# One exponential over both decay blocks, earlier splits, norms and p projection, and three PSUM banks for each of two uses

## The chip, the cores and the metric

The kernel runs on one core of a Trainium2 chip. The metric is the device time of one execution in microseconds (us), smaller is better. The engines named below are PE (TensorE, matrix products), PEld (its weight loads), DVE (VectorE), ACT (ScalarE), POOL (GpSimd) and SP (SyncE, which issues most of the DMAs). Each engine runs its own instructions in the order in which they stand and waits, where it must, for semaphores of the others.

## The reference

One layer of a hybrid decoder over 1024 tokens of width 1024, in float32: a Mamba-2 mixer, a mixture of 64 experts in 8 groups, a per-layer embedding that is projected and gated, and a last RMS norm. Cut to what matters here:

```python
u = rms_norm(x);  z, xBC, dt = split(u @ w_in)            # 1024 x 5152
x, B, C = split(silu(causal_conv4(xBC) + conv_b))          # 32 heads of 64, 4 groups, state 128
acum = cumsum(dt * A) within chunks of 128 tokens
decay = exp(acum[l] - acum[s]) for s <= l;   decay_in = exp(acum)
y = (C B^T * decay) @ (x dt) + (C * decay_in) @ state_in   # then the state goes on to the next chunk
h = x_in + (group_rms_norm((y + D x) * silu(z)) * gnorm) @ w_out
h = h + moe(rms_norm(h))         # top-1 group, top-2 experts in it, gated MLPs with 512 hidden
gate = sigmoid(rms_norm(h) @ ple_w_gate + ple_b_gate)
h = h + gate * (p @ ple_w_proj)  # p: 1024 x 256, ple_w_proj: 256 x 1024
out = rms_norm(h)
```

## The kernel before

**The mixer** (`ssd`, from the start to about 640 us). The tokens are taken in two halves `hf` of 512, and in each the four groups `g` one after the other, which makes eight units. A unit projects ten column tiles t = 0 to 9 of `w_in`: B, C, four of x and four of z. A tile is 128 columns by 512 tokens, made as three products of split float32 operands (`xh wh`, `xl wh`, `xh wl`; L204 to L206) over eight blocks of the inner dimension, so 24 matmuls into a PSUM tile "mm". The weights are split just ahead of them in `proj` by L69 and L70: `wh` is a rounded copy on ACT, `wl` the rest on DVE. `conv_tile` then copies the product out (L278) and runs the convolution, three passes on DVE (L284).

Woven between the tiles of a unit is the scan of the unit before, four chunks c of 128 tokens. The dictionary `plan` says after which tile each step is written: `front(0)`, `front(1)`, `back(0)`, `front(2)`, `back(1)`, `front(3)`, `back(2)` and `back(3)` at t = 0, 1, 2, 3, 4, 5, 6 and 8. A `front` loads the cumulated steps of 8 heads, broadcast to all partitions, from the DRAM scratch `acd` into `ac` (L322, 512 KB), and makes two blocks of 128x1024: `ec` = exp(ac) (L338), and, after `ac` has had each row's own value taken off it in place (L340, eight instructions on DVE), `ac` = exp(ac) (L342). The first, times C (L348), weighs the incoming state; the second, times the masked C B^T (L352), weighs the chunk's own inputs. A `back` multiplies both on PE (L369, L371) into "py", and DVE takes "py" on into `yz` (L382, L384). `ac` has three buffers and `ec` two.

`x_half(hf)` loads the tokens, sums their squares, takes the reciprocal root, spreads it over the columns by a turn on PE (L177), loads the transposed columns, and splits them into `xh` and `xl`. For the second half it is written into t = 3 to 7 of the last unit of the first half. Turned tiles and small products use PSUM tiles "tp"; there are four banks for "mm" and two for "tp".

**The output product and the router** (`out_router`, about 640 to 880 us). It multiplies by `w_out`, and routes the tokens in blocks (`stats`, `turn`, `logits`, then the three parts of `route`: `first`, `second`, `third`). At its end nothing but the last block's routing is left: the counts on PE (L685 to L690, tile "pa"), two packings (L714), a gather of token rows by DMA, and the first spreading products of the experts' stage (L1017, `pc<-S,uh`).

**The experts** (`moe`, about 880 us to the end). Eight groups g are taken in turn. Their weights come in blocks of 1 MB, issued by SP through a ring of buffers and a few spare ones (`yx`, `vx`, `ring2`), and PE multiplies them (L1027, tiles "pgate", "pup", "py"). The per-layer embedding of finished tokens (`ple`) is woven into the next group by `fill`: nine times 128 rows. For each, 1 KB rows of `p` are gathered, turned by PE in two transposes (`turn_p`, L855), and projected half by half (`project_p`, L861); the gate's product is L908. In the group g = 6 two more such projections are written early (`project`), for the last two sets of rows.

Instructions are recorded by a framework that puts each engine's instructions in an order of its own, by priorities; a place in the text does not fix the place in a queue, except under `manual_schedule`.

Of the kernel before, what the change touches and what calls it, by code (L numbers as in the profile page):

```python
# [17 lines left out]
T, D = 1024, 1024  # L18
# [23 lines left out]
class K:  # L42
# [64 lines left out]
    def ssd(self, left, right):  # L107
# [35 lines left out]
        def x_half(hf):  # L143

            ss, rs, *tmp = (wk.tile([128, HC], F32, name=n) for n in ("rs", "rs", "nt0", "nt1", "nt2"))
            cols = []

            def columns():
                for j in range(2):
                    w = wraw.tile([128, KD, 256], F32, name="w").rearrange("p a b -> p (a b)")  # L150
                    w = w.rearrange("p (k t) -> p k t", t=HT)
                    nc.sync.dma_start(w, a["xT"].rearrange("(k p) t -> p k t", p=128)[:, 4 * j:4 * j + 4,
                                                                                      hf * HT:(hf + 1) * HT])
                    cols.extend(w[:, k] for k in range(4))

            for i in range(HC):
                t = hf * HC + i
                xt = (wk.tile([128, D], F32, name="ec") if i == 3 else wk.tile([128, D], F32, name="ac", bufs=3))
                nc.sync.dma_start(xt, a["x"][t * 128:(t + 1) * 128, :])
                if i == HC - 1:  # L160
                    if hf == 0:
                        W.append(load(2 * DI, 2 * DI + 512))
                    columns()
# [14 lines left out]
            rsb = wk.tile([128, HT], F32, name="dT", bufs=1)  # L178
            nc.scalar.activation(rsb, pr.rearrange("p c t -> p (c t)"), AF.Copy)

            def scale(k):
                nc.vector.tensor_mul(cols[k], cols[k], rsb)
# [4 lines left out]
            yield  # L187
# [75 lines left out]
        def proj(w, i, x):  # L263
            wh = wsp.tile([128, KD, 128], F32R, name="wh")
            wl = wsp.tile([128, KD, 128], F32R, name="wl")
            self.split(wh, wl, w[:, :, i * 128:(i + 1) * 128])
            ps = self.ps_mm.tile([128, 512], F32, name="mm")
            mm3(ps, wh, wl, x)
            return ps

        def conv_tile(hf, w, i, x, m):
# [5 lines left out]
            ps = proj(w, i, x)  # L277
# [11 lines left out]
        def project(hf, g):  # L289
            x = X[hf]  # L290
            w = W.pop() if W else load(2 * DI + g * 128, 2 * DI + 512 + g * 128)
            xT, zT = [], zp.tile([128, 4, HT], F32, name="z")
            bT = conv_tile(hf, w, 0, x, 16 + g)
            yield
            cT = conv_tile(hf, w, 1, x, 20 + g)
            U[hf, g] = bT, cT, xT, zT
            yield
            for j in range(2):
                w = load(DI + g * 512 + j * 256)
                for i in range(2):  # L300
                    xT.append(conv_tile(hf, w, i, x, 4 * g + 2 * j + i))
                    yield
            for j in range(2):
                w = load(g * 512 + j * 256)
                for i in range(2):
                    nc.scalar.activation(zT[:, 2 * j + i], proj(w, i, x), AF.Silu)
                    yield

        def scan(hf, g):
# [6 lines left out]
            def front(c):  # L316
# [4 lines left out]
                ac = wk.tile([128, 8, Q], F32, name="ac", bufs=3)  # L321
                nc.sync.dma_start(ac, bass.AP(tensor=acd.tensor, offset=acd[8 * g:8 * g + 1, cg * Q:cg * Q + 1].offset,  # L322
# [89 lines left out]
        X, SZ, U, W = {}, {}, {}, []  # L412
        for i, _ in enumerate(x_half(0)):
# [1045 lines left out]
```

## Time and profile before

| what | value |
|---|---|
| median of 3 runs | 1950.36 us (1946.88 to 1954.07) |
| profiled execution, its own time | 1954.31 us |
| span from its first to its last instruction | 1952.4 us |
| mean granted clock of TensorE | 0.982 of full |
| PE busy | 1848.3 us (95%) |
| DVE busy | 1031.5 us (53%) |
| ACT busy | 749.5 us (38%) |
| moved by DMA | 538.39 MB |

The shares of busy time are means over three stages with different limits, so the profile is read stage by stage: the mixer, the output product with the router, the experts.

### The profile page before, as it was taken

The numbers are of one execution on the slowest core, as the hardware profiler recorded it, in microseconds if no ns is written. First come the engines' busy times: TensorE is split into PE (matmuls) and PEld (weight loads), VectorE is DVE, ScalarE is ACT, GpSimd is POOL, SyncE is SP. The second block draws the span as 40 slices with busy tenths as digits, with TensorE's granted clock in tenths as the row PEclk, the third lists the DMA queues.
The fourth block names the chain that finished last, engine by engine and source line by source line (L and its number), as shares of the span: only waits on it lengthen the run. The fifth ranks groups of instructions, "written<-read, shape, count | busy, mean of one in ns | idle before, by whom it ended". The sixth has DMA issues, their size and how long they took to land.

```text
span 1952.4 us, 23158 instructions
## 1 busy us (share of the span) xinstructions
PE 1848.3 (95%) x8702; PEld 1047.1 (54%) x8702; DVE 1031.5 (53%) x2194; ACT 749.5 (38%) x1040; POOL 182.7 (9%) x276
## 2 busy tenths in 40 slices
PE   6999997999999999979999999999999999999996
PEld 4778775777887678863343333433433334334334
DVE  5497896858988876573341514423325244143223
ACT  5476766557767533322021211312222113122223
POOL 1011110201111031021000000000000000000004
PEclk9999998999999999988999999999999999999998
DMA  7425444345442787956999999999999999998883
GB/s 220 118 75 137 115 134 127 88 97 134 110 110 53 243 294 238 346 195 254 422 421 394 401 421 385 412 412 383 420 382 404 420 373 423 404 375 325 337 322 109
DMA packets 192166, 538.39 MB, mean 276 GB/s; under 512 B 16046, under 2 KB 128688, under 8 KB 143920
## 3 DMA queue, kind: packets, MB, share of 16 engines
q1 hardware_dynamic: 177744, 514.21, 72.0%
q10 hardware_dynamic: 11008, 12.94, 2.0%
q0 software_dynamic: 3296, 9.70, 1.3%
q8 instruction: 70, 1.15, 0.2%
q14 instruction: 48, 0.39, 0.1%
HBM read 520.95 MB, written 17.69 MB: 276 GB/s over the span
## 4 chain that ended last, share of the span: by engine, by line
PE 81%; DMA 7%; DVE 7%; ACT 2%; issue 2%; POOL 1%; SPq 0%; POOLq 0%; ACTq 0%; DVEq 0%
PE pup L1027 11%; PE pgate L1027 11%; PE py L1027 10%; PE mm L206 6%; PE mm L204 6%; PE mm L205 6%; PE pq L908 6%; PE pc L1017 3%; PE mm L505 2%; PE mm L506 2%; PE mm L507 2%; DMA w<-in_w_up_dram 2%; PE pc L861 2%; DMA ac<-acd 2%; PE pc L1090 2%
## 5 line engine op out<-in xcount | busy, mean ns | idle before, releaser
L204 PE MATMUL mm<-xh,wh 128*128 128x512 f32 x640 | 265.6, 415 | 3.3 <-ACT xh L197 2.2
L206 PE MATMUL mm<-xh,wl 128*128 128x512 f32 x640 | 254.5, 400 | 8.4 <-DVE wl L70 8.3
L205 PE MATMUL mm<-xl,wh 128*128 128x512 f32 x640 | 253.9, 397 | 0.3 <-DVE xl L198 0.3
L1027 PE MATMUL pup<-w,XT 128*64 128x512 f32 x1016 | 239.1, 598 | 1.6 <-DMA w<-in_w_up_dram 1.6
L1027 PE MATMUL pgate<-w,XT 128*64 128x512 f32 x1000 | 232.7, 599 | 0.0
L1027 PE MATMUL py<-w,hT 128*64 128x512 f32 (+1 forms) x1024 | 227.1, 586 | 2.1 <-DMA w<-in_w_down_dram 2.1
L70 DVE TENSOR_TENSOR yx<-py,yx 128x512 fp32r<-128x512 f32 (+1 forms) x68 | 44.8, 659 | 234.2 <-ACT yx L69 234.2
L1027 PEld LDWEIGHTS py<-w,hT 128*64 128x64 f32 x1024 | 70.0, 137 | 146.2 <-issue 138.2
L1027 PEld LDWEIGHTS pup<-w,XT 128*64 128x64 f32 x1016 | 72.1, 136 | 141.9 <-issue 131.5
L206 PEld LDWEIGHTS mm<-xh,wl 128*128 128x128 f32 x640 | 122.6, 192 | 38.5 <-DVE wl L70 12.2
L204 PEld LDWEIGHTS mm<-xh,wh 128*128 128x128 f32 x640 | 122.9, 192 | 34.2 <-issue 4.5
L1027 PEld LDWEIGHTS pgate<-w,XT 128*64 128x64 f32 x1000 | 68.7, 137 | 134.2 <-issue 129.6
L205 PEld LDWEIGHTS mm<-xl,wh 128*128 128x128 f32 x640 | 123.0, 192 | 29.9 <-issue 4.3
L908 PE MATMUL pq<-wpg,vx 128*128 128x512 f32 x256 | 123.1, 607 | 0.0
L70 DVE TENSOR_TENSOR wl<-w,wh 128x1024 fp32r<-128x1024 f32 x80 | 97.4, 1220 | 46.4 <-ACT wh L69 46.4
L69 ACT ACTIVATE wh<-w 128x1024 fp32r<-128x1024 f32 x80 | 84.3, 1054 | 72.0 <-PE mm L205 59.4
L284 DVE SCALAR_TENSOR_TENSOR xbc<-raw,convw,xbc 128x512 f32<-128x512 f32 x144 | 109.7, 762 | 3.8 <-ACT xbc L282 2.7
L506 PE MATMUL mm<-wl,yh 128*128 128x512 f32 x256 | 99.3, 398 | 2.0 <-DVE wl L517 1.9
L505 PE MATMUL mm<-wh,yh 128*128 128x512 f32 x256 | 96.0, 402 | 4.8 <-ACT yh L69 4.6
L69 ACT ACTIVATE yx<-py 128x512 fp32r<-128x512 f32 (+1 forms) x68 | 38.9, 572 | 159.4 <-PE py L1027 159.4
L1058 ACT ACTIVATE hT<-pt 128x512 f32<-128x512 f32 x31 | 18.4, 593 | 211.5 <-PE pt L1056 211.5
L507 PE MATMUL mm<-wh,yl 128*128 128x512 f32 x256 | 98.0, 393 | 0.0
(360 smaller groups left out, 2815.6 us busy)
## 6 DMA issues: line engine op xcount, KB each, us to landing
w<-in_w_up_dram SPq DMA_DIRECT2D x127, 1024.0 KB, 9.5
w<-in_w_gate_dram SPq DMA_DIRECT2D x125, 1024.0 KB, 9.1
w<-in_w_down_dram SPq DMA_DIRECT2D x120, 1024.0 KB, 9.5
w<-in_w_in_dram SPq DMA_DIRECT2D x32, 1024.0 KB, 5.6
w<-in_w_out_dram SPq DMA_DIRECT2D x48, 512.0 KB, 5.2
ac<-acd SPq DMA_DIRECT2D x32, 512.0 KB, 9.3
w<-in_w_in_dram SPq DMA_DIRECT2D x16, 512.0 KB, 8.7
yn<-yz SPq DMA_DIRECT2D x32, 256.0 KB, 4.4
```

Of the source, the lines that this page charges most:

```text
L69: self.nc.scalar.activation(dst_h, src, AF.Copy)
L70: self.nc.vector.tensor_sub(dst_l, src, r_(dst_h))
L204: nc.tensor.matmul(ps, lhsT=wh[:, k], rhs=x[0][:, k], start=(k == 0), stop=False)
L205: nc.tensor.matmul(ps, lhsT=wh[:, k], rhs=x[1][:, k], start=False, stop=False)
L206: nc.tensor.matmul(ps, lhsT=wl[:, k], rhs=x[0][:, k], start=False, stop=(k == KD - 1))
L284: nc.vector.scalar_tensor_tensor(o, raw[:, j:j + HT], convw[:, m, j:j + 1], o, op0=OP.mult, op1=OP.add)
L505: nc.tensor.matmul(po[i][hf], lhsT=yh[:, ts], rhs=wh[:, cs], start=(k == 0), stop=False)
L506: nc.tensor.matmul(po[i][hf], lhsT=yh[:, ts], rhs=wl[:, cs], start=False, stop=False)
L507: nc.tensor.matmul(po[i][hf], lhsT=yl[:, ts], rhs=wh[:, cs], start=False, stop=(k == 15))
L908: nc.tensor.matmul(V["pq"], lhsT=V["vT"][:, k], rhs=wpg[:, k, cs], start=(k == 0), stop=(k == KD - 1))
L1017: nc.tensor.matmul(px, lhsT=x[:, k], rhs=G.S[:, i], start=(i == 0 and x is u[i][0]), stop=(i == 1 and x is u[i][1]))
L1027: nc.tensor.matmul(ps[64 * b:64 * b + 64], lhsT=xt(k0 + k, b), rhs=w[b][:, k, cs], start=(k0 + k == 0), stop=(k0 + k == K - 1))
```

## The change

1. **One exponential.** `ac` and `ec` become the two halves of one tile `ae`, with two buffers in place of three and two. The load goes to the `ec` half, the eight subtractions write the `ac` half from it, and one ACT instruction over 128x2048 takes both exponentials.
2. **Early splits.** A generator `weights()` writes the split of tile m+1 right after the matmuls of tile m, ahead of its convolution.
3. **Early norms.** The sum of squares and the reciprocal root are a function of their own, `norms(hf)`; that of the second half is written into t = 2 to 6 of the first unit, and its result is kept in `RB`. `x_half(1)` keeps the load of columns, the scaling and the split, at t = 6 and 7 of the last unit of the first half. A scan's norm and store move from t = 0 and 2 to t = 1 and 3.
4. **Early p projection.** All of `p @ ple_w_proj` is made at the end of `out_router`, in 16 pieces (two float32 matmuls of 128x512 and an ACT copy each), in a PE order written by hand around the last routing steps; eight DMAs store it to the DRAM scratch `ppd`. The experts' stage gathers rows of 4 KB from there and makes no projection; `turn_p`, `project_p` and the two early projections in g = 6 go, as does the tile `wpp`.
5. **PSUM.** "mm" has three banks and "tp" three.

```diff
-                ac = wk.tile([128, 8, Q], F32, name="ac", bufs=3)
-                nc.sync.dma_start(ac, bass.AP(tensor=acd.tensor, ...
+                ae = wk.tile([128, 2, 8, Q], F32, name="ae")
+                ec, ac = ae[:, 0], ae[:, 1]
+                nc.sync.dma_start(ec, bass.AP(tensor=acd.tensor, ...
...
-                ec = wk.tile([128, 8, Q], F32, name="ec")
-                nc.scalar.activation(ec, ac, AF.Exp)
                 for h in range(8):
-                    nc.vector.tensor_scalar(ac[:, h], ac[:, h], acs[:, c, 8 * g + h:8 * g + h + 1], 0.0,
+                    nc.vector.tensor_scalar(ac[:, h], ec[:, h], acs[:, c, 8 * g + h:8 * g + h + 1], 0.0,
                                             op0=OP.subtract, op1=OP.min)
-                nc.scalar.activation(ac, ac, AF.Exp)
+                nc.scalar.activation(ae, ae, AF.Exp)
...
+            wh, wl = ahead.pop() if ahead else next(W)
             ps = self.ps_mm.tile([128, 512], F32, name="mm")
             mm3(ps, wh, wl, x)
+            ahead.extend(w for w in [next(W, None)] if w)
             return ps
...
+                if hf == 0:
+                    rows = norms(1)
+                    for t in (2, 3, 4, 5, 6):
+                        at(t, next, rows)
             if before:
-                at(0, before[2])
-                at(2, before[3])
+                at(1, before[2])
+                at(3, before[3])
...
-                for t in (3, 4, 5, 6, 7):
+                for t in (6, 7):
                     at(t, next, xg)
...
+        pieces = project()
+        with tc.manual_schedule(engines={mybir.EngineType.PE}):
+            for f in side[:-3]:
+                f()
+            for n, f in zip((6, 0, 0), side[-3:]):
+                f() if f is not side[-1] else f(lambda n: [next(pieces, None) for _ in range(n)])
+                for _ in range(n):
+                    next(pieces)
+            for _ in pieces:
+                pass
...
-            self.gather(self.p0, self.a["p"], g)
+            self.gather(self.p0, self.ppd, g)
...
-            nc.vector.tensor_mul(gt, gt, self.project_p(V["pT"], hf, pc_) if pr is None else pr[:, cs])
+            nc.vector.tensor_mul(gt, gt, pr[:, cs])
...
-                    early = [project(vx[:, 1792:], nxt.pr), project(self.p0, cur.pr)]
...
-        self.ps_mm = self.pool("ps_mm", 4, PSUM, ps)
-        self.ps_tp = self.pool("ps_tp", 2, PSUM, ps)
+        self.ps_mm = self.pool("ps_mm", 3, PSUM, ps)
+        self.ps_tp = self.pool("ps_tp", 3, PSUM, ps)
```

How the instructions stand on the engines that this concerns. First, SP's queue around the scan's loads in the second half of the mixer, where the scan of the second-to-last group begins (`ac` and `ae` are the loads, `w` those of `w_in`). Before:

```order
L322 DMA ac_4451<-acd_98 128x8x128
L322 DMA ac_4729<-acd_98 128x8x128
L260 DMA w_4833<-in_w_in_dram 128x8x256
L322 DMA ac_4800<-acd_98 128x8x128
L260 DMA w_4989<-in_w_in_dram 128x8x256
L260 DMA w_5129<-in_w_in_dram 128x8x256
L322 DMA ac_4956<-acd_98 128x8x128
```

Here `ac_4729` to `ac_4956` are the loads of chunks 0, 1 and 2; with three buffers, `ac_4956` takes the buffer of `ac_4451`, the last chunk of the scan before. After:

```order
L334 DMA ae_4659<-acd_98 128x8x128
L260 DMA w_5034<-in_w_in_dram 128x8x256
L334 DMA ae_4752<-acd_98 128x8x128
L260 DMA w_5162<-in_w_in_dram 128x8x256
L334 DMA ae_4906<-acd_98 128x8x128
```

With two buffers, `ae_4906`, chunk 2 again, takes the buffer of `ae_4659`, chunk 0 of the same scan, which is read by the products of `back(0)`.

Next, DVE in the same place, from the end of `back(0)` (its result is py_4888 before, py_4823 after) on. Before:

```order
L382 SCALAR_TENSOR_TENSOR yz_4908<-xbc_4445,dsk_104,py_4888 128x128
L340 TENSOR_SCALAR ac_4956<-ac_4956,acs_2820 128x128
L384 TENSOR_TENSOR yz_4908<-yz_4908,z_4020 128x512
L340 TENSOR_SCALAR ac_4956<-ac_4956,acs_2820 128x128 x7
L346 COPY ed_4983<-ec_4972 128x8
L70 TENSOR_TENSOR wl_4994<-w_4989,wh_4993 128x1024
```

After:

```order
L392 SCALAR_TENSOR_TENSOR yz_4843<-xbc_4401,dsk_104,py_4823 128x128
L350 TENSOR_SCALAR ae_4906<-ae_4906,acs_2774 128x128
L394 TENSOR_TENSOR yz_4843<-yz_4843,z_3980 128x512
L350 TENSOR_SCALAR ae_4906<-ae_4906,acs_2774 128x128 x7
L375 TENSOR_TENSOR st_4975<-st_4821,ed_4777 128x512
L415 TENSOR_TENSOR yz_4203<-yz_4203,tp_4893 128x512
L415 TENSOR_TENSOR yz_4357<-yz_4357,tp_4893 128x512
L415 TENSOR_TENSOR yz_4487<-yz_4487,tp_4893 128x512
L415 TENSOR_TENSOR yz_4576<-yz_4576,tp_4893 128x512
L344 TENSOR_TENSOR xc_4916<-tp_4908,dt_s_2773 128x512
L70 TENSOR_TENSOR wl_4965<-w_4880,wh_4964 128x1024
```

In both, the eight subtractions on the chunk's load stand right behind the rows on the result of `back(0)`; after the change the split of the next tile's weights (`wl_4965`) stands some six instructions behind them.

Last, PE at the end of the router. Before, the last logits are followed by the counts, and the last packing by the spreading products:

```order
L618 MATMUL tp<-wr,uT 128x72 x8
L612 MATMUL tp<-ident,h 128x128 x8
L618 MATMUL tp<-wr,uT 128x72 x8
L688 LDWEIGHTS tris
L688 MATMUL tp<-M,tris 128x72
```

After, six pieces of the p projection stand there:

```order
L667 MATMUL tp<-wr,uT 128x72 x8
L661 MATMUL tp<-ident,h 128x128 x8
L667 MATMUL tp<-wr,uT 128x72 x8
L594 MATMUL mm<-w,wh 128x512 x12
L737 LDWEIGHTS tris
L737 MATMUL tp<-M,tris 128x72
```

Two more pieces stand ahead of each packing, and the last six between the second packing and the spreading products:

```order
L764 LDWEIGHTS at
L764 MATMUL tp<-oms,at 128x104
L594 MATMUL mm<-w,wh 128x512 x12
L1048 MATMUL pc<-S,uh 128x512 x2
L1048 MATMUL pc<-S,ul 128x512
```

So 32 matmuls have moved from the experts' stage to a place between the last logits and the first spreading product. On SP the loads of their operands stand behind the first weights of the experts, and the eight stores to `ppd` ahead of three more weight blocks (`ring2`, `yx` and `vx`).

## Rows read from the trace of the kernel before

**Rows 1.** Busy time of each engine in stretches of the span (start and end in us, length, then PE, PEld, DVE, ACT, POOL busy with the number of instructions; at the end the granted clock of TensorE as a share of full, the busy share of the DMA engines, and GB/s).

```profile
20.00:633.00 613.00, 581.11 (x3144) 459.22 (x3143) 478.54 (x987) 403.23 (x492) 91.00 (x155) 0.97 0.43 111
290.00:331.00 41.00, 27.48 (x132) 21.38 (x131) 25.80 (x76) 24.42 (x30) 3.03 (x4) 0.83 0.40 112
320.00:330.00 10.00, 6.71 (x21) 5.22 (x22) 7.50 (x18) 9.08 (x14) 1.84 (x2) 0.66 0.23 72
450.00:600.00 150.00, 150.00 (x856) 120.01 (x855) 130.13 (x261) 107.80 (x130) 24.00 (x28) 1.00 0.44 111
860.00:890.00 30.00, 15.75 (x80) 9.78 (x81) 21.25 (x82) 7.87 (x14) 9.92 (x19) 0.66 0.40 137
950.00:1000.00 50.00, 47.26 (x200) 22.24 (x198) 18.14 (x28) 10.22 (x16) 0.00 (x0) 1.00 1.01 421
1226.00:1354.00 128.00, 127.03 (x530) 47.43 (x528) 44.02 (x84) 29.10 (x46) 3.41 (x3) 1.00 1.00 403
```

**Rows 2.** What PE waited for in the mixer, 20 to 640 us (waiting tile and line, releaser, us in total, times, longest).

```profile
PE mm L206 <- DVE wl L70: 8.3, 8, 2.2
PE tp L177 <- DVE rs L66: 7.8, 1, 7.8
```

**Rows 3.** The timeline at the two longest of PE's waits (start us, duration us, engine, line, operation; in brackets the idle time before it and its releaser).

```profile
297.92 1.06 ACT L170 ACTIVATE sq<-ec 128x1024 bf16<-128x1024 f32 x1 [6.04 <-DMA ec<-in_x_dram]
301.67 1.09 PE L177 MATMUL tp<-ident,rs 128*128 128x128 f32 x4 [7.80 <-DVE rs L66]
...
317.70 0.39 PE L205 MATMUL mm<-xl,wh 128*128 128x512 f32 x1
...
318.61 0.39 PE L206 MATMUL mm<-xh,wl 128*128 128x512 f32 x1
319.61 1.06 ACT L338 ACTIVATE ec<-ac 128x1024 f32<-128x1024 f32 x1 [7.23 <-DMA ac<-acd]
...
322.04 3.16 ACT L197 ACTIVATE xh<-w,gk 128x512 fp32r<-128x512 f32 x5
...
323.29 0.59 PE L394 MATMUL tp<-ones,sqs 128*128 128x1 f32 x2 [4.29 <-POOL sqs L389]
```

**Rows 4.** Groups of instructions on DVE between 450 and 600 us (line, operation, shapes, count, busy us, mean ns of one, idle before).

```profile
L284 DVE SCALAR_TENSOR_TENSOR xbc<-raw,convw,xbc 128x512 f32<-128x512 f32 x40 | 30.0, 751 | 0.5 <-issue 0.3
L70 DVE TENSOR_TENSOR wl<-w,wh 128x1024 fp32r<-128x1024 f32 x21 | 25.5, 1217 | 7.6 <-ACT wh L69 7.6
L340 DVE TENSOR_SCALAR ac<-ac,acs 128x128 f32<-128x128 f32 x64 | 17.9, 342 | 0.3 <-ACT ec L338 0.3
L348 DVE TENSOR_TENSOR ec<-ec,xbc 128x1024 f32<-128x1024 f32 x9 | 11.0, 1218 | 0.1
L382 DVE SCALAR_TENSOR_TENSOR yz<-xbc,dsk,py 128x128 f32<-128x128 f32 x33 | 9.8, 340 | 3.5 <-PE py L371 3.5
```

**Rows 5.** Groups of instructions on ACT between 20 and 640 us, the exponentials, their table loads and the copy of a split, in the same columns.

```profile
L69 ACT ACTIVATE wh<-w 128x1024 fp32r<-128x1024 f32 x78 | 82.2, 1054 | 69.4 <-PE mm L205 59.4 <-issue 9.7
...
L342 ACT ACTIVATE ac<-ac 128x1024 f32<-128x1024 f32 x30 | 31.8, 1060 | 10.0 <-DVE ed L346 7.2 <-DVE ac L340 2.5
L338 ACT ACTIVATE ec<-ac 128x1024 f32<-128x1024 f32 x30 | 31.7, 1058 | 26.6 <-DMA ac<-acd 26.3
...
L338 ACT ACT_TABLE_LOAD x20 | 25.7, 1283 | 0.7 <-DMA ac<-acd 0.4
```

**Rows 6.** The scan's loads (line L322): who waited for them (us in all, times), and the time from issue to landing.

```profile
  ACT ec L338: 26.3, 5
...
DMA to landing us min/median/max: 7.7/9.3/15.1
```

**Rows 7.** PE's timeline at the end of the router (columns as in Rows 3): the last logits, the counts, the two packings, the first spreading product, and the first group's own first matmul.

```profile
862.39 2.00 PE L618 MATMUL tp<-wr,uT 128*128 128x72 f32 x16
868.82 0.22 PE L688 MATMUL tp<-M,tris 128*128 128x72 bf16 x1 [4.42 <-DVE me L664]
...
872.51 0.33 PE L714 MATMUL tp<-omi,at 128*128 128x16 bf16 x6 [2.76 <-DVE at L706]
874.27 0.70 PE L714 MATMUL tp<-oms,at 128*128 128x104 bf16 x6 [1.43 <-DVE oms L728]
879.77 1.22 PE L1017 MATMUL pc<-S,uh 128*128 128x512 f32 x2 [4.80 <-ACT uh L1003]
...
889.76 2.80 PE L1027 MATMUL pgate<-w,XT 128*64 128x512 f32 x12
```

**Rows 8.** The matmuls of the p projection and the turns ahead of it, all of the experts' stage (columns as in Rows 4).

```profile
L861 PE MATMUL pc<-wpp,vx 128*128 128x512 f32 x72 | 36.3, 627 | 5.0 <-ACT vx L856 2.5 <-DVE ha L1092 1.3 <-DVE hb L1092 1.3
...
L855 PE MATMUL pc<-ident,p 128*128 128x128 f32 x16 | 3.2, 280 | 0.4 <-DVE ha L1092 0.3
```

**Rows 9.** The first matmuls of the groups g = 1, 6 and 7 of the experts' stage (line L1027, tile "pgate"; durations min, median, max in ns, then the start of the first and of the last of them in us).

```profile
L1027 PE MATMUL pgate<-w,XT x4: 592/618/643, 1005.1 to 1005.6; 128*64 128x512 f32 x4
L1027 PE MATMUL pgate<-w,XT x4: 592/618/643, 1644.7 to 1645.2; 128*64 128x512 f32 x4
L1027 PE MATMUL pgate<-w,XT x4: 592/618/643, 1784.9 to 1785.4; 128*64 128x512 f32 x4
```

**Rows 10.** A load of 512 KB by SP in the router's stage (the page's list of DMA issues: count, KB each, median us to landing).

```profile
w<-in_w_out_dram SPq DMA_DIRECT2D x48, 512.0 KB, 5.2
```

More of the change, by code (lines that the diff above doesn't have):

```diff
@@ L141, in small_loads, with norms @@
             nc.sync.dma_start(al, bcast_rows(a["a_log"], 128, 0, NH))
-        def x_half(hf):
+        def norms(hf):
             ss, rs, *tmp = (wk.tile([128, HC], F32, name=n) for n in ("rs", "rs", "nt0", "nt1", "nt2"))
[L146 to L154, printed above, removed]
             for i in range(HC):
                 t = hf * HC + i
-                xt = (wk.tile([128, D], F32, name="ec") if i == 3 else wk.tile([128, D], F32, name="ac", bufs=3))
+                if i % 2 == 0:
+                    two = wk.tile([128, 2, D], F32, name="ae")
+                xt = two[:, i % 2]
                 nc.sync.dma_start(xt, a["x"][t * 128:(t + 1) * 128, :])
[L160 to L163, printed above, removed]
                 if hf == 0 and i % 2:
@@ L410, in scan @@
             return front, back, norm, store
-        X, SZ, U, W = {}, {}, {}, []
-        for i, _ in enumerate(x_half(0)):
+        X, SZ, U, RB = {}, {}, {}, {}
+        first, xg = norms(0), x_half(0)
+        for i in range(HC):
+            next(first)
             if i == 0:
                 nc.sync.dma_start(gk, a["ssd_norm_kp"])
-            if i == HC - 1:
-                small_loads()
+        ahead.append(next(W))
+        next(xg)
+        small_loads()
+        next(first)
+        next(xg)
         sizes = step_sizes(0)
@@ L476, in out_router @@
         self.gdd = dp.tile([128, 8, NE], F32, name="gdd")
+        self.ppd = dp.tile([T, D], F32, name="ppd")
         macc = self.macc
@@ L509, in out_router @@
             for i in range(n):
-                po.append([(self.ps_mm if i < 2 else self.ps_m2).tile([128, 512], F32, name="mm") for _ in range(2)])
+                po.append([(self.ps_m2 if i == 2 else self.ps_tp if i == hf == 1 else self.ps_mm).tile(
+                    [128, 512], F32, name="tp" if i == hf == 1 else "mm") for hf in range(2)])
             for k in range(16):
@@ L1281, in moe @@
                 if g == NGR - 2:
-                    nxt.pr, cur.pr = self.h0[(g + 2) % 3], self.ho[(SET[g] - 1) % 3]
-                    fill[2].append(lambda: self.gather(vx[:, 1792:], a["p"], g + 1))
-                    early = [project(vx[:, 1792:], nxt.pr), project(self.p0, cur.pr)]
-                    for n, x in ((17, 0), (18, 0), (20, 1), (21, 1)):
-                        fill.setdefault(n, []).append(lambda x=x: next(early[x]))
+                    nxt.pr = self.h0[(g + 2) % 3]
+                    fill.setdefault(17, []).append(lambda: self.gather(nxt.pr, self.ppd, g + 1))
                 if nxt:
```

142 lines of the change are left out of this document (76 added, 66 removed).

## The prediction

> **What bounds the kernel now.** I read the stretches first, then the waits of PE in the stretches that are not full, then the timeline at the longest of them. PE is the bound nearly everywhere: in the middle of the mixer it is busy for all of 150 us, and for 127.03 of 128 us in a group of the experts' stage [rows 1]. There is something to gain in three places. In the mixer, from 20 to 633 us, PE is busy for 581.11 of 613 us at 0.97 of its clock [rows 1]: 31.9 us idle, and up to 18 us (0.03 x 613) lost to the clock, of which I take 12, since part of the half clock lies in idle time; 44 together. At the end of the router it works 15.75 of 30 us, at 0.66 [rows 1]. And in the experts' stage PE itself is what is short, but the DMA engines are as full: share 1.00, 403 GB/s [rows 1].
>
> **The p projection, in the experts' stage.** What goes is 72 matmul records of 36.3 us and 16 turns of 3.2 us [rows 8]: 39.5 us for nine sets, 4.4 each, with waits of 5.0 us ahead of them. Groups 1 to 5 last (1644.7 - 1005.1) / 5 = 127.9 us, group 6 140.2 [rows 9]. PE alone would allow 127.9 - 4.4 = 123.5 us. The DMAs move 403 x 128 = 51.6 MB in a group, and the gathered rows grow from 1 to 4 KB for 128 tokens, 0.4 MB more. At the best rate that a stretch shows, 421 GB/s [rows 1], 52.0 MB take 123.5 us. Both bounds meet there, and two queues that are both full don't hide each other perfectly: I take 3.3 us a group, between 4.4 and 1.7 (412 GB/s, halfway between 403 and 421), so -16.5 for five. Here a page speaks: the Trainium skill, "DMA: Bandwidth & Descriptors", section "Where 436 GB/s comes from", puts the ceiling of the fabric at about 435 GB/s. By it the DMAs would need an estimated 119.5 us and PE's 4.4 us would count in full, five more us in the sum; no stretch of this trace reaches it, and 421 decides. Group 6 also loses the two early projections (8.8 us) and part of the waits: 140.2 would become some 124.7, so -15.5. Group 7 has one set, -4.2. Group 0 has no projection and gathers two sets of longer rows while the DMAs are what it waits for (421 GB/s at 47.26 of 50 us of PE [rows 1]): 0.8 MB, +1.9. Sum **-34** (-26 to -40).
>
> **The p projection, at the end of the router.** 32 matmuls of two records come back, 16 pieces of 4 x 0.504 = 2.0 us [rows 8], 32 us. What do they fill? The last logits end at 864.4, the first spread starts at 879.77, the group's own products at 889.76 [rows 7]. The operands of the pieces use buffers that the last output products free at 859, and a load of 512 KB takes 5.2 us [rows 10], so the first piece can start at about 865. Six pieces (12 us) end at 877; the counts, which were ready at 868.8, wait for that. From there DVE needs 2.76 and 1.43 us to each packing [rows 7], which two pieces (4 us) cover: second packing at 886, six more pieces to 898. The gather that follows the packing took 879.77 - 874.27 = 5.5 us to the first spread [rows 7], and is now covered by 12. The spreads start at 898 at full clock and not at half, so they need about 5 us in place of 10: own products at some 903, **+13** (+9 to +18). So 32 us of work cost 13, since 13.4 us of idle time and 5 of clock are filled. The last stores to `ppd` hold three weight blocks back on SP's queue to about 898; before, the DMA engines have nothing to do there either (share 0.40 [rows 1]), and the ring's first reload waits for the same products. If that cover fails, 3 MB at 421 GB/s, 7 us.
>
> **The mixer, what it gains.** The stretch of `norms(1)`: PE waits 7.80 us at 301.67 because a token load came late [rows 3]; its half clock behind it costs some 2 more. Both go, since the norms are made 200 us earlier: -10. The change of halves, 318.6 to 323.3, goes only in part (below). The early splits attack the 8.3 us in 8 waits for `wl` [rows 2]. The third "tp" bank and the split ahead of the convolution may take some 4 us of short waits. The single exponential itself brings nothing directly: two of 1.06 us and a table load of 1.283 [rows 5] on an engine that is busy for 107.8 of 150 us [rows 1], with no wait of PE behind it in that stretch. In all -17 if nothing else happened.
>
> **The mixer, what it costs.** Here the change adds a wait. With two `ae` buffers the load for `front(c+2)` can be issued only when the products of `back(c)` are through, and it takes 9.3 us (7.7 to 15.1) to land [rows 6]. Before, with three buffers, it was issued a `back` earlier, and only five loads were waited for at all, 26.3 us on ACT [rows 6]. The order shows where the wait falls: the eight subtractions stand on DVE right behind the rows on the result of that same `back(c)`. DVE needs 4 x 0.3 us (spacing of L382), a product and perhaps a split of 1.2 until it gets there [rows 4], some 3 us, and then stands still for 5 to 6 us in each `front`. Behind it are queued the split `wl` of the next tile and, on ACT, the exponential and behind it `wh`. DVE is busy for 130.13 of 150 us there [rows 1], so of a unit's 71 us (150 us for the 21 splits of L70, ten in a unit [rows 4]) it can lose 9.
>
> One full unit, followed by hand with these durations. A tile is 24 matmuls at (318.61 - 317.70) / 4 = 0.2275 us, 5.46 us [rows 3]; what is left of 71 us, 17, is four `front`, four `back` and the norm, of which I give a `back` 1.7. Zero is the end of the last `back` of the scan before.
> - `front(0)`: load lands at 9.3, subtractions to 11.0, `wl` of the next tile but one at 12.2, just in time for PE at 12.9. Nothing lost.
> - `front(1)`: its load is released by the next `back`, at 12.9, lands at 22.2; subtractions to 23.9, table load and exponential on ACT to 27.3, then another table load, a copy out and `wh` to 30.2. PE has been out of work since 24.8: 5.4 lost.
> - `front(2)`: released at 44, landed at 53.3, subtractions and the norm's products on DVE, `wl` at 59.8 where PE wants it at 58.1: 1.7 lost.
> - `front(3)`: DVE is late by now and reaches the next `wl` at 70.5, wanted at 66.3: 4.2 lost.
>
> That is 11.3 us for a unit, and 8.6 with the shortest landing. The replay starts with DVE right behind PE; where it has a lead, less is lost. I take 8 for the four ordinary units with a whole scan, 4 for two that carry less, 40 together. At the change of halves the load of the first chunk is again issued late and `xl` stands behind it on DVE: about 12 us of idle time and 2 of clock, 14, where the stretch of 290 to 331 now loses 13.5 and clock [rows 1]. The second pass through `acd` has a `wl` behind a wait, 8. Other short waits 3. Sum 65 in place of 44: **+21**. Its ends: with DVE's waits hidden throughout, -17; with 11 us in six units and a clock loss behind each wait of over 4 us, as at 320 to 330 us (0.66 [rows 1]), +50.
>
> **The sum.** -34 + 13 + 21 = 0 against the profiled execution's 1954.31 us (span 1952.4), which lies 4 us above the median of 1950.36. So my forecast is no change, 1951 us; 0.5%, about what a measurement of this kernel can tell from no change, is 9.8 us.
>
> **Rivals.**
> (a) *The mixer keeps its lead, the rest counts.* DVE's waits fall into its idle 13%, or its lead over PE is larger than I gave it. For it: the split is now one tile ahead, 7 us of cover for a 5 us wait, and PE shows no wait at all from 450 to 600 us [rows 1]. Then -34 + 13 - 17 = -38: about 1913; half of it, 1932. Chance 0.32, from 1908 to 1940.
> (b) *The two buffers bind.* Slower: each `front` pays the landing of its load through DVE and ACT, and the idle times of 5 us drop the clock. Decided by whether a wait outlasts the one tile (7 us) of lead that the early split gives: replayed above, two of four do. The sum is -34 + 13 + 44 = +23, about 1974, up to 1985. The Trainium skill speaks against the change in the same way: "DMA: Bandwidth & Descriptors", section "Rules for kernel authors", advises to issue a DMA early, compute, and wait late; the row with 26.3 us of waits in five of 32 loads [rows 6] agrees that early issues hide these loads. Chance 0.28.
> (c) *The DMAs bind the experts' stage.* If the rate stays at the 403 GB/s of a whole group, 52.0 MB take 129 us, so groups 1 to 5 gain nothing: 17 us less gain, about 1968 with the rest as forecast. Against it speak 421 GB/s over 50 us, and that PE is busy for 127.03 of 128 us of such a group [rows 1], so the DMAs were not pressed. Chance 0.05.
> My forecast has 0.35, within 0.5% of 1950.4: the two large rivals differ from it by one term, the mixer's, in opposite directions.
>
> **How the numbers follow.** Faster by over 0.5%: (a) and a little of the forecast's lower end, 0.33. Within: the forecast, 0.35. Slower: (b) and (c), less what the weak forms of both leave within 0.5%, 0.32. The range reaches from the middle of (a) to the far end of (b): 1914 to 1984. For the likeliest case alone it would be 1941 to 1960.
>
> **What would show it.** In the changed kernel's profile: group starts some 124.6 us apart and no early pair in group 6 (right if 123.5 to 126); the first product of group 0 at 903 plus whatever the mixer shifts; in the mixer, waits of DVE for the DMA of `ae` of 4 to 6 us, several in each unit, and waits of PE for `wl` or `wh` well over the 8.3 us of before. If DVE waits for `ae` but PE doesn't wait for the splits, (a) is right. If PE's busy share from 450 to 600 us falls below 0.9, (b) is. If the groups stay at 127 us with the DMA share at 1.00, (c) is. The forecast would be wrong, too, if the pieces of the p projection started late because their operands land late.

## The result, and the profile after

The changed kernel takes 1965.07 us (median of 4 runs, 1964.36 to 1965.99), the kernel before 1950.2 in the same series: a ratio of 1.0076, with a 95% interval of 1.0057 to 1.0095. It is slower by 0.8%, within the range that was given (1914 to 1984) and outside the 0.5% that the forecast called no change: by sign it is the case that had been given 0.32, and it lies between the forecast (1951) and rival (b) (1974). The profiled execution has a span of 1963.0 us, 10.6 more than that of before; this difference is taken apart here. (By the medians it is 15; the profiled execution of before lay 4 us above its median.)

First the busy time in the stretches of [rows 1] that answer, of the changed kernel, in the same columns; the third and the fourth are the end of the router and one group of the experts' stage:

```profile
20.00:633.00 613.00, 574.73 (x3117) 454.18 (x3117) 463.47 (x970) 349.90 (x425) 85.87 (x153) 0.97 0.42 110
450.00:600.00 150.00, 141.88 (x819) 114.71 (x818) 114.47 (x241) 87.07 (x103) 21.51 (x27) 0.98 0.43 104
860.00:890.00 30.00, 29.47 (x182) 23.91 (x181) 23.99 (x80) 8.19 (x13) 3.34 (x6) 1.00 0.57 197
1169.70:1295.10 125.40, 123.24 (x515) 46.74 (x514) 44.15 (x84) 27.86 (x44) 3.00 (x3) 1.00 1.01 414
```

PE, which had no idle time from 450 to 600 us, has 8.1 there; its busy share of 0.946 stays above the 0.9 that was named as the sign of rival (b). What it waits for, and what DVE waits for, from 20 to 660 us, where [rows 2] and [rows 6] had 8.3 us for `wl` and five waits of ACT for the load:

```profile
PE mm L206 <- DVE wl L70: 16.7, 12, 3.4
PE mm L204 <- ACT wh L69: 12.9, 3, 6.4
PE mm L525 <- ACT yh L69: 12.9, 1, 12.9
```

```profile
DVE ae L350 <- DMA ae<-acd: 75.2, 22, 8.2
...
DVE ed L356 <- ACT ae L352: 20.1, 10, 3.3
```

DVE now stands still 22 times for the scan's load, 3.4 us each time, and the splits behind it are late for PE. The third row of PE holds the longest single wait; the kernel before had less of it:

```profile
PE mm L505 <- ACT yh L69: 4.6, 2, 3.7
```

The timeline there, at the passage from the mixer to the output product:

```profile
642.22 1.66 DVE L350 TENSOR_SCALAR ae<-ae,acs 128x128 f32<-128x128 f32 x8 [6.28 <-DMA ae<-acd]
...
643.95 1.28 ACT L352 ACT_TABLE_LOAD   x1 [7.25 <-DVE ae L350]
645.24 1.91 ACT L352 ACTIVATE ae<-ae 128x2048 f32<-128x2048 f32 x1
645.25 1.36 ACTq L540 DMA_DIRECT2D y<-yn  x3
...
651.04 0.40 ACT L69 ACTIVATE yh<-y 128x256 fp32r<-128x256 f32 x1
...
651.49 0.80 PE L525 MATMUL mm<-wh,yh 128*128 128x512 f32 x1 [12.91 <-ACT yh L69]
```

It is read downward: the load of the last scan's second chunk lands at 642.2, the subtractions and the exponential follow, and only behind the exponential, on ACT's own queue, come the DMAs that fetch the gated rows `y`. PE starts at 651.5, where it started at 642.6 before.

The end of the router and the start of the experts' stage, PE's timeline, for [rows 7]:

```profile
886.37 2.00 PE L667 MATMUL tp<-wr,uT 128*128 128x72 f32 x16 [0.31 <-ACT uT L662]
888.21 10.51 PE L594 MATMUL mm<-w,wh 128*128 128x512 f32 x24
...
906.17 0.44 PE L764 MATMUL tp<-oms,at 128*128 128x104 bf16 x6
...
915.98 3.70 PE L594 MATMUL mm<-w,wh 128*128 128x512 f32 x8 [2.44 <-ACT wl L596]
920.64 0.73 PE L1048 MATMUL pc<-S,uh 128*128 128x512 f32 x2 [0.96 <-DVE S L1001]
...
928.60 1.94 PE L1058 MATMUL pgate<-w,XT 128*64 128x512 f32 x8
```

and the starts of the groups 1, 6 and 7, for [rows 9]:

```profile
1044.79 3.65 PE L1058 MATMUL pgate<-w,XT 128*64 128x512 f32 x16
...
1672.08 3.65 PE L1058 MATMUL pgate<-w,XT 128*64 128x512 f32 x16
...
1798.54 3.65 PE L1058 MATMUL pgate<-w,XT 128*64 128x512 f32 x16
```

From these starts the difference of 10.6 us comes apart as follows (before and after, us; the last matmul of the logits starts at 864.1 and at 888.1):

| stretch | before | after | difference | predicted |
|---|---|---|---|---|
| start to the last logits (mixer, output product) | 864.1 | 888.1 | +24.0 | +21 |
| last logits to the first group's own run of products | 25.7 | 40.5 | +14.8 | +13 |
| group 0 | 115.3 | 116.2 | +0.9 | +1.9 |
| groups 1 to 5 | 639.6 | 627.3 | -12.3 | -16.5 |
| group 6 | 140.2 | 126.5 | -13.7 | -15.5 |
| group 7 and the end | 167.5 | 164.5 | -3.0 | -4.2 |

### The profile page after: what moved, and what is told of

It reads as the page before. It is cut to its first block, busy times and chain, and to the rows that moved or that the text cites. A ratio compares the mean times of both kernels' runs of the same rounds, so it can differ in the third digit from the quotient of the medians.

```text
span 1963.0 us, 23062 instructions
## 1 busy us (share of the span) xinstructions
PE 1842.2 (94%) x8676; PEld 1050.7 (54%) x8676; DVE 1022.8 (52%) x2194; ACT 703.0 (36%) x979; POOL 179.0 (9%) x276
## 5 line engine op out<-in xcount | busy, mean ns | idle before, releaser
L1058 PE MATMUL pup<-w,XT 128*64 128x512 f32 x1016 | 244.1, 598 | 4.8 <-DMA w<-in_w_up_dram 4.6
L1058 PEld LDWEIGHTS pup<-w,XT 128*64 128x64 f32 x1016 | 77.7, 136 | 141.5 <-issue 118.9
L350 DVE TENSOR_SCALAR ae<-ae,acs 128x128 f32<-128x128 f32 x256 | 59.3, 299 | 83.8 <-DMA ae<-acd 83.8
L525 PE MATMUL mm<-wh,yh 128*128 128x512 f32 x208 | 81.3, 410 | 13.0 <-ACT yh L69 12.9
L526 PE MATMUL mm<-wl,yh 128*128 128x512 f32 x208 | 82.7, 401 | 7.6 <-DVE wl L538 7.6
```

Of the source, the lines that this page charges most:

```text
L350: nc.vector.tensor_scalar(ac[:, h], ec[:, h], acs[:, c, 8 * g + h:8 * g + h + 1], 0.0, op0=OP.subtract, op1=OP.min)
L525: nc.tensor.matmul(po[i][hf], lhsT=yh[:, ts], rhs=wh[:, cs], start=(k == 0), stop=False)
L526: nc.tensor.matmul(po[i][hf], lhsT=yh[:, ts], rhs=wl[:, cs], start=False, stop=False)
L1058: nc.tensor.matmul(ps[64 * b:64 * b + 64], lhsT=xt(k0 + k, b), rhs=w[b][:, k, cs], start=(k0 + k == 0), stop=(k0 + k == K - 1))
```

## The experiments

The theory at the start: the p projection brings some 13 us, the early norms and splits 16 to 17, and the joined block `ae` with its two buffers takes more than both, since the load starts late. The rivals: the loss sits in the PSUM banks or the moved norms; or the gain of the experts' stage is held back by PE and not by the DMAs. The kernel before was run again beside the experiments and took 1952.7 to 1954.4 us (medians), against 1950.2 beside the changed kernel. Differences in us between an experiment and the changed kernel are therefore sure to some 4 us; the ratios go by the kernel before of the same series.

**One part taken back, one part alone.** The old scan step (`ac` with three buffers, `ec` with two, two exponentials) in the changed kernel:

```diff
-                ae = wk.tile([128, 2, 8, Q], F32, name="ae")
+                ac = wk.tile([128, 8, Q], F32, name="ac", bufs=3)
...
+                ec = wk.tile([128, 8, Q], F32, name="ec")
+                nc.scalar.activation(ec, ac, AF.Exp)
...
-                nc.scalar.activation(ae, ae, AF.Exp)
+                nc.scalar.activation(ac, ac, AF.Exp)
```

> The changed kernel with the scan step of before put back (three buffers for the load, two exponentials); all its other parts stay. Theory: the two buffers are what the change pays for, in the mixer and above all at the start of the output product, where PE waited 12.9 us for a token block whose load stands behind the late exponential. Then the time from the last tile of the mixer to the last logits falls from 250 us to about 232, the mixer ends 10 us or more earlier than 638, and the run takes 1925 to 1938 us. Rival: the 19 us that the output stage lost come from the PSUM banks (three for products, one product borrowing a bank of the turned tiles) or from the moved norms; then that stage stays at 245 to 250 us and the run takes 1948 to 1960 us.

It took 1920.63 us (0.9828 of before, 0.9814 to 0.9843), 44 less than the changed kernel and less than the theory's range. Its last logits start at 848.1 us: 16 earlier than before, 40 earlier than after. So the joined block costs 40 us by the last logits, and everything else in that stretch gains 16. Where the 40 us lie is seen in the mixer (from 20 us to the start of its last matmul) and in the output stage (from there to the last logits), first of the changed kernel, then of this run, in the columns of [rows 1]:

```profile
20.00:638.20 618.20, 579.93 (x3140) 458.45 (x3139) 466.42 (x976) 351.28 (x427) 87.07 (x155) 0.97 0.42 110
638.20:888.10 249.90, 225.47 (x1185) 182.28 (x1184) 168.32 (x410) 95.82 (x131) 32.67 (x47) 0.97 0.72 249
20.00:606.00 586.00, 568.42 (x3140) 452.90 (x3139) 474.28 (x977) 406.12 (x493) 91.73 (x153) 0.99 0.44 117
606.00:848.10 242.10, 224.60 (x1186) 181.50 (x1184) 169.12 (x410) 95.11 (x133) 34.54 (x49) 0.98 0.74 255
```

The mixer carries 32 of them: 21 are idle time of PE, and some 11 are longer matmuls, at a granted clock of 0.97 against 0.99. The output stage carries 8. It takes 242 us here and not the 232 of the theory, and PE waits 9.8 us for `yh` at its start with the old scan step too, so the joined block adds only 3 us to that wait.

The reverse, the joined block alone in the kernel before (the same edit turned round):

> The kernel before with one part alone: the joined block with two buffers and one exponential. Theory: without early splits and early norms the whole price shows, some 20 us in the mixer and 15 to 20 us at the start of the output product, so 1980 to 1992 us. Rival: the price lies in the combination with the other parts (banks, splits one tile ahead); alone it is 1945 to 1955 us.

2055.79 us, 1.0538 of before (1.0523 to 1.0552). Both expectations missed it: 103 us, far over the 40 that the joined block costs in the changed kernel. That the early splits hide the greater part there, as they give the next tile's weights one tile of lead, is an argument and was not tried apart: this run lacks the early norms and the new banks as well. Its mixer lasts to 714.8 us, and up to the output product PE waits 38.7 us for `wl` and 18.4 for `wh`.

The p projection alone, the old mixer around it (`ssd` and the PSUM banks as before, the rest as after):

> The kernel before with one part alone: the p projection at the end of the router. Theory: the end of the router grows by 13 us, the experts' stage shrinks by 26, so 1935 to 1939 us; groups 1 to 5 last 125.4 us each as in the changed kernel. Rival: the stage's gain came from the later start (weights further ahead) and not from the work taken out; then the groups last 127 us and the run takes 1950 us or more.

1938.11 us, 0.9926 (0.9913 to 0.994): -14.8 us. The groups 1 to 5 last (1648.5 - 1022.0) / 5 = 125.3 us. The theory holds, and the projection is worth about the same beside either mixer (in the changed kernel 14.8 - 28.1 = -13.3 us).

**The passage to the output product.** The loads of `y` issued by POOL:

```diff
-                nc.scalar.dma_start(y[:, :n * 128], self.yn[...
+                nc.gpsimd.dma_start(y[:, :n * 128], self.yn[...
```

> The changed kernel with the loads of the output product's token blocks issued from POOL's queue and not from ACT's. Theory: they no longer stand behind the exponential that waits for the scan's load, so the wait of 12.9 us ahead of the first output product falls under 6 us and the run is 5 to 9 us shorter, 1956 to 1960 us. Rival: the first product waits for its split weights on ACT and DVE, which stand behind the same exponential; then the wait stays at 10 us or more and the time at 1963 to 1967 us.

1969.4 us, no shorter, and the wait for `yh` is still 12.1 us. My theory fell: the DMAs' place in ACT's queue is not by itself what makes the first product late. The copy into `yh` stands behind the late exponential as well, and the trace of that run shows that this decides there:

```profile
641.29 1.91 POOL L540 DMA_DIRECT2D y<-yn  x3 [0.39 <-issue]
...
646.34 1.28 ACT L352 ACT_TABLE_LOAD   x1 [6.78 <-DVE ae L350]
...
652.38 0.40 ACT L69 ACTIVATE yh<-y 128x256 fp32r<-128x256 f32 x1
```

The loads are issued 4 us earlier than in the changed kernel, but ACT first waits 6.8 us for the subtractions, then works without a pause up to the copy, and has no wait for `y`.

**Buffers or place?** Three joined buffers, with room from one buffer less for convolved tiles and for gated rows:

```diff
-                ae = wk.tile([128, 2, 8, Q], F32, name="ae")
+                ae = wk.tile([128, 2, 8, Q], F32, name="ae", bufs=3)
```

> The changed kernel with three buffers for the joined block in place of two; the room comes from one buffer less each for convolved tiles (13) and for gated rows (5). Theory: the number of buffers is the cause, not the joining; the load is issued one step earlier again, DVE's waits for it fall from 75 us in 22 to under 30, and the run takes what the kernel with the old scan step took, 1916 to 1928 us. Rival: the single exponential itself, whose subtractions now stand ahead of everything on ACT, costs the time; then DVE's waits fall but PE's waits for split weights stay near 30 us, and the run takes 1945 us or more. If it takes less than 1915, the joining is worth something once the buffers are there.

1956.21 us (1.0007 of before, 0.9993 to 1.0021): only 9 us better than two (13 by the ratios), and DVE still waits for the load, from 20 to 640 us, where the changed kernel has 68.9 us in 21 waits:

```profile
DVE ae L350 <- DMA ae<-acd: 65.0, 19, 8.0
```

The theory that the number of buffers is the cause fell, and of the rival the time came, but DVE's waits hardly fell. The mixer gained nothing (its last matmul starts at 637.7 us, against 638.2); what there is to gain came behind it. The timeline of that run shows a load on SP's queue and the subtractions whose wait it ends:

```profile
499.08 0.37 SPq L334 DMA_DIRECT2D ae<-acd  x1
508.64 1.07 DVE L350 TENSOR_SCALAR ae<-ae,acs 128x128 f32<-128x128 f32 x5 [3.62 <-DMA ae<-acd]
```

The subtractions end their wait 9.6 us after the issue, a landing's length; so even with a third buffer they stood that close behind the load that they read there. A control with the old scan step and the same smaller numbers of the other buffers:

> A control: the kernel with the old scan step, with one buffer less each for convolved tiles (13) and gated rows (5), as in the run with three joined buffers. Expected the same as without that, 1918 to 1924 us; if it takes 1945 us or more, the three joined buffers were judged wrongly, by what had to make room for them.

1919.0 us (0.9817, 0.9796 to 0.9837): those buffers cost nothing.

The place, then. The subtractions held on DVE behind the step's masking product, which waits for PE's turned tiles; two buffers as in the change:

```diff
+                held = nc.vector.tensor_mul(cbm, pb[:, 1], self.tri)
...
+                with tc.issue_after(held.ins):
+                    for h in range(8):
+                        nc.vector.tensor_scalar(ac[:, h], ec[:, h], ...
```

> The changed kernel, two buffers and one exponential, with one thing added: the eight subtractions of a step are queued on DVE behind that step's own masking product (the one into cbm), which waits for PE's turns of the step. Theory, formed after the third buffer had brought only 9 us: it is not the number of buffers but the place in the queue. The subtractions are the first reader of the load and stand right behind the products that let the load start, so DVE stands still for its landing; held back, they come one tile (some 7 us) later. DVE's waits for the load fall from 75 us to under 35, and the run takes 1925 to 1945 us. Rival: with two buffers the load itself is too late whatever stands where; then DVE's waits fall but PE waits for the decay blocks instead, and the run takes 1960 us or more.

1934.3 us (0.9895, 0.9876 to 0.9914): one line of order takes back 31 of the 44 us. In this run neither DVE nor ACT has a wait for the load left in the mixer, whose last matmul starts at 605.3 us, as with the old scan step (606.0), and not at 638.2. So in the mixer two buffers are enough, and the single exponential changes its length by less than 1 us. What remains, 14 us by the last logits, lies in the output stage:

```profile
20.00:605.30 585.30, 571.31 (x3140) 449.54 (x3139) 461.45 (x965) 356.19 (x428) 84.61 (x155) 1.00 0.45 116
605.30:862.60 257.30, 231.28 (x1185) 185.38 (x1184) 172.31 (x421) 95.54 (x130) 33.40 (x47) 0.94 0.71 242
```

That stage takes 257 us, against 242 with the old scan step and 250 in the changed kernel: PE idles 8.5 us longer than with the old scan step, and its matmuls take 6.7 us longer at a granted clock of 0.94 against 0.98. Its wait at the start of the output product, 10.9 us, is only 1 us over the 9.8 of that run.

The old order of work on the joined tile with two buffers (the load goes to the `ac` half, first exponential on ACT, subtractions in place):

```diff
-                nc.vector.tensor_scalar(ac[:, h], ec[:, h], ...
-                nc.scalar.activation(ae, ae, AF.Exp)
+                nc.scalar.activation(ec, ac, AF.Exp)
+                nc.vector.tensor_scalar(ac[:, h], ac[:, h], ...
+                nc.scalar.activation(ac, ac, AF.Exp)
```

> The changed kernel with its joined blocks and two buffers, but the old order of work in them: the first exponential on ACT reads the load, the subtractions work in place, a second exponential follows. Theory (place in the queue): the first reader is on ACT again, DVE's subtractions come later, so most of the 44 us between the changed kernel and the one with the old scan step comes back, 1925 to 1940 us. Rival (number of buffers): with two buffers it stays at 1955 us or more, and ACT takes over the waits for the load.

2006.88 us (1.0282, 1.0261 to 1.0303), 42 us worse than the change. As I had put it, this went against the theory of the place; the waits tell how. ACT is now the first reader, just as close behind the load, and what stands behind it there are the copies `wh`:

```profile
ACT L349 <- DMA ae<-acd: 91.1, 15, 9.0
```

```profile
DVE ae L351 <- ACT ae L349: 96.0, 21, 9.2
```

Both engines stand still, one after the other. The first reader's distance from the load counts, on whichever engine it is. But this run and the old scan step have the same order of work and differ in the tiles alone, and lie 86 us apart; with that order the buffers do count. They set when a load can start, and the order sets how soon after that its first reader stands. That the old scan step has its distance by its tiles, as its first exponential writes into `ec`, which has buffers of its own, was argued and not tried apart, and the old order with three joined buffers was not run. The old scan step is not free of such waits: ACT has six of them, 24.2 us in all, from 20 to 640 us.

The subtractions moved to POOL:

```diff
-                    nc.vector.tensor_scalar(ac[:, h], ec[:, h], ...
+                    nc.gpsimd.tensor_scalar(ac[:, h], ec[:, h], ...
```

> The changed kernel, two buffers, with the eight subtractions of each step on POOL in place of DVE. Theory: the price is that DVE stands still with the next split behind it; POOL has nothing behind the wait, so PE's waits for DVE's split (16.7 us) fall under 8 us and the run takes 1930 to 1948 us, unless POOL's slower instructions hold up the exponential. Rival: the chain of load, subtraction, exponential and product over two buffers is itself too long; then PE waits as long for other releasers and the run takes 1960 us or more.

2097.31 us (1.0737, 1.0714 to 1.0761), slower than anything else. It can't decide between the theories, for POOL is too slow at this (20 to 700 us):

```profile
L350 POOL TENSOR_SCALAR ae<-ae,acs 128x128 f32<-128x128 f32 x208 | 170.8, 841 | 112.4 <-DMA ae<-acd 92.8 <-PE tp L342 9.4 <-PE py L381 6.0
```

0.84 us for each of the eight, where DVE takes 0.34 [rows 4], and ACT waits 113.5 us for them in 21 waits from 20 to 640 us.

Both remedies, three buffers and the held subtractions:

> Both remedies at once: the changed kernel with three joined buffers (13 and 5 buffers for convolved tiles and gated rows) and the subtractions held behind the masking product. Theory: the price needs both an early load and a reader that stands late; with both, DVE's waits for the load nearly vanish (under 15 us) and the run takes what the old scan step takes, 1912 to 1922 us; the single exponential is worth 5 us at most, since nothing waits for ACT there. Rival: the single exponential and its saved table loads are worth more once nothing hides them, 1900 to 1911 us; or the third buffer adds nothing to holding back, 1930 to 1936 us.

1928.32 us (0.9877, 0.9856 to 0.9897): 6 us better than held alone, and 9 us behind the control with the old scan step. DVE's waits for the load vanish as expected, but the time lies between the ranges of the theory and of its rival. The runs side by side (start of the mixer's last matmul, length of the output stage to the last logits, start of the last logits, us):

| run | mixer's last matmul | output stage | last logits |
|---|---|---|---|
| before | 633.4 | 230.7 | 864.1 |
| the change | 638.2 | 249.9 | 888.1 |
| old scan step | 606.0 | 242.1 | 848.1 |
| three buffers | 637.7 | 245.1 | 882.8 |
| held back | 605.3 | 257.3 | 862.6 |
| three buffers, held back | 605.9 | 249.5 | 855.4 |
| old order, two buffers | 679.6 | 249.9 | 929.5 |

Holding back takes 33 us out of the mixer, and the output stage is 7 us longer with it. The third buffer does nothing for the mixer and takes 5 to 8 us out of the output stage. So the single exponential, freed of its price in the mixer, brings nothing to be seen there; what it would bring in the output stage without the hold was not tried apart.

**The banks, and the experts' stage.** The old scan step with four banks for products and two for turned tiles:

> The kernel with the old scan step and all other parts, but with four banks for products and two for turned tiles as before the change. Theory: early splits and norms bring most of the 16 us that this kernel gains ahead of the last logits, the banks 4 us or less: 1920 to 1926 us. Rival: the third bank for turned tiles is what lets the scan's steps slip in; then 1930 to 1936 us.

1919.23 us (0.982, 0.9802 to 0.9838), against 1920.63 with three and three: no difference. The early splits and norms bring all of the 16 us (with the small moves that go with them); the two were not tried apart.

Projected rows of 256 columns in place of 1024, the other columns left out:

```diff
-        self.ppd = dp.tile([T, D], F32, name="ppd")
+        self.ppd = dp.tile([T, PD], F32, name="ppd")
...
-            self.gather(self.p0, self.ppd, g)
+            self.gather(self.p0[:, 0:PD], self.ppd, g)
```

> The changed kernel, storing and gathering only 256 of the 1024 columns of the projected rows (the other columns of the projection are left out), so 0.4 MB less per group to move. Theory: the experts' groups are held by the DMAs at 125.45 us; they fall by 0.9 us or more each, the run by 6 to 9 us, 1956 to 1959 us. Rival: they are held by PE's own waits and order; then the groups stay at 125.2 to 125.6 us and the run at 1963 to 1966 us.

1955.19 us, 10 less than the changed kernel, with the groups 1 to 5 at (1661.9 - 1042.1) / 5 = 124.0 us in place of 125.45. The work of PE in these groups is the same in both (2561 matmul records), so the DMAs hold them.

## Why the prediction was right, and what in it was off

*The sum.* Predicted 0, measured +10.6 on the profiled executions; by the medians the forecast of no change was missed by 14 us. The measured time lies in the range because the range reaches from the one rival to the other, 70 us; the likeliest case (1941 to 1960) did not come. The signs of all terms held. Each of the three large ones was too favourable, by 3, 2 and 6 us, and that is the whole miss. That they came so near is in part luck: inside two of them errors cancelled.

*The experts' stage* (-34, measured -28.1) is the step that was most mis-sized. The bounds were right in kind, but the groups last 125.45 us, not 124.6 (still within the 123.5 to 126 that were named as the sign of the forecast). The DMAs move 411 to 414 GB/s over a whole group and not 421, and the run with narrow rows shows that it is they who bind: it gets back 1.5 us a group. Rival (c) so took a part of the gain, though not at its 403 GB/s. The page's ceiling of 435 GB/s (the Trainium skill, "DMA: Bandwidth & Descriptors", section "Where 436 GB/s comes from") was rightly set aside: the stretches of before and after that are full stay at 402 to 421 here.

*The end of the router* (+13, measured +14.8). The order came as worked out: the pieces run from 888.2 to 919.7, the routing steps and the gather fall behind them, and the clock is at full from 860 to 890. The sizes came less well. The pieces took 28.7 us and not 32. Against that stand two waits that were not foreseen, 2.44 us ahead of the last pieces and 0.96 us ahead of the spreads, and the spreads themselves: they were to run at full clock and take 5 us, but the granted clock fell to 0.50, its lower level, from 923 to 925 us, right behind these waits and one more of 1.16 us, and from their start to the group's own products it is 8.0 us (920.6 to 928.6), where it was 10.0 before.

*The mixer's gain* (-17): -16 in the run with the old scan step, but not from where it was expected. That run's mixer is 27 us shorter, and its output stage 11 us longer, than before. Within the mixer the wait for the token load went, but PE still waits 8.5 us in seven waits for `wl`, against 8.3 in eight: the early splits did not take these waits away. About 13 us came from shorter matmuls, at a granted clock of 0.99 against 0.97, where the working had given the clock some 2. The banks, given 4 us with the split's new place, brought nothing. What makes the output stage longer stays open in the main; PE's wait at its start, 9.8 us in place of 3.7, is the largest single part.

*The mixer's cost* (+38 against that gain): +40 by the last logits, 32 of them in the mixer, where the working had put them. The mechanism was the one replayed, DVE behind the load with the split and the exponential behind it: PE's waits for `wl` and `wh` have the predicted size, up to 3.4 and 6.4 us, and when the first reader is held back the mixer is as short as with the old scan step. DVE's waits were fewer and shorter than replayed, 22 of 3.4 us on average and not one of 5 to 6 in each `front`, and 11 of the 32 us came through the clock, which the working had, but for some 2 us, at its upper end only. Against before the changed mixer is just 4.8 us late, since gain and cost nearly cancel there; of the 19 us that the output stage has more than before, 11 come with the old scan step as well and 8 with the joined block.

*Rival (b)*, the two buffers, was named for the wrong half. It is true that the load starts late with two buffers, but a third one alone takes back 9 us, none of it in the mixer, and holding back the first reader takes back 31 with two. The sentence of the Trainium skill that was cited there ("DMA: Bandwidth & Descriptors", section "Rules for kernel authors": issue early, wait late) has two halves; here the second one, to wait late, was worth some three times the first.

*Not foreseen*: how much the other parts of the change hide. Without them the same joined block costs 103 us; which of them hides it was not tried apart.

The best version that was run is the one with all parts but the joined block: 1919 to 1921 us in its three forms, 1.7 to 1.8% faster than before and 2.3% faster than the change.

## What to carry to other kernels

When a buffer is joined or dropped, look at who reads the load first, on which queue, and how many instructions stand between the event that lets the load start and that reader; if it is less than a landing, all that is queued behind the reader waits too. Here the framework's own order put the reader there with two buffers and with three, and one line of explicit order brought more than a third buffer. Such a line has a price of its own elsewhere, so the stretches are compared one by one, and against the run with the part taken back, not against before alone. Several edits in one change can hide each other's worth: here one lost some 40 us and the others gained some 30, and only taking single parts back showed it.

## What the runs showed that was not expected

The subtractions of 128x128 took 0.84 us each on POOL against 0.34 us on DVE [rows 4] (means). And behind three waits of 1 to 2.4 us PE's granted clock fell to its lower level for the spreading products, in a stretch that had been planned at full clock. And 0.4 MB less to gather in a group shortened it by 1.5 us, where 0.4 MB at 413 GB/s are 1.0 us; the rate over the five groups was also higher, 415 GB/s against 412, for a reason that no run shows.
